# Scaling both banks of a projection pair at once, copying keys earlier, and two longer pauses, in a hybrid decoder block

## The chip, the cores and the metric

The kernel runs on one core of a Trainium2 chip. The metric is the device time of one execution in microseconds (us), the median of three runs of the same program. TensorE (PE) does the matrix products, VectorE (DVE) and ScalarE (ACT) the elementwise work, GpSimd (POOL) issues most of the small copies, and SyncE (SP) issues the weight transfers. Matrix products write to PSUM, which has eight banks; everything else lives in SBUF.

## The reference

A block of a language model on 256 tokens with 16 learned "meta" tokens ahead of them, T = 272 in all, width 2048. One wide projection feeds two branches: gated DeltaNet (16 heads of 128) and forgetting attention (16 heads of 128). Their outputs are mixed by per-channel sigmoid gates, projected, added to the input, and followed by a squared-ReLU MLP of width 8192.

```
u = rms_norm(h, mix_norm_g)
p = u @ w_in                                   # q, k, v | z | b, a | fox q, k, v | f | gate_a, gate_b
qkv = silu(causal_depthwise_conv(p[q, k, v]))  # four taps for each channel
beta, g = sigmoid(b), -exp(a_log) * softplus(a + dt_bias)
w = solve(tril(beta * k k^T * decay) + 1, ...) # the inverted triangular blocks, per head
o = chunked_gated_delta_rule(q, k, v, g, beta)
y_b = forgetting_attention(fox q, k, v, f)
h = h + (sigmoid(gate_a) * (y_a @ w_o_gdn) + sigmoid(gate_b) * (y_b @ w_o_fox)) @ w_out
h = h + square(relu(rms_norm(h) @ w_up)) @ w_down
```

All of it is float32, and the kernel keeps that precision by splitting each operand in a high and a low part.

## The kernel before, in words

The weights are read once, in pieces of 1 MB (`load`, L138, on SP's queue; three buffers). Each half piece is split: ACT writes the high part `wh` (L130, shown as L82), DVE the low part `wl` (L131). PE multiplies three times for each tile of 128 rows and 128 columns: high by high, high by low, low by high (L168 to L170). A pair of 256 columns, two heads, is 96 such products, in two PSUM banks `acc` out of a pool of four. So the pair after next writes to the banks of this pair, and can start only when they have been read.

For q, k and v that reader is `ca` (L465): DVE multiplies the bank by the row `RU` (one over the norm of each token) and writes SBUF. ACT and DVE then do the four taps of the convolution (L466, L470) and the SiLU (L472).

All the small work (convolutions, gates, key products, the triangular inversion, the heads of the delta rule) is written as generators that stand in a list. After each k-tile of a projection `pump()` advances each of them by one `yield`; `pause(n)` waits n k-tiles. So the text of the kernel gives an order of instructions. The kernel is then built with a scheduler that places the instructions anew on each engine by its own costs, so a pause moves instructions by more or less than its count. Each engine runs its own list strictly in order, and an instruction that waits holds back all that stand behind it on its engine.

The places that the change touches:
- `small_columns` (L321): the 48 columns for beta, decay and forget gate (`rawS`), 48 narrow products L338 to L340, then `gates` (L378), with the ten tiny cumulative sums L414 to L423.
- `key_pair` (L612): two heads of keys: convolution, products k k^T (L625, L628), sums of squares (L631, L634).
- `invert` (L518): the diagonal blocks are inverted on DVE (`substitute`), go through DRAM (`dY`) and back, and are joined by small products from L552 on.
- `query_pair` (L695), and `value_head` (L737), one for each of the 16 heads. A value head takes the convolved `vt`, copies it with POOL to `vb` and a part of `kT` to `kb` (`bits`, L90), transposes them on PE (`flip`, L94), and runs a chain of small products: L771, L777, L785, and twice L791, L792, L799, L806. `V` (L758) scales the transposed values. There are 29 such small products for a head, 58 for a pair.

Temporary tiles come from pools by size: ten of 128 columns (`kb` among them), twelve of 272 (`ca`, `cv`, `vt`, `vb`), four of 512.

Of the kernel before, what the change touches and what calls it, by code (L numbers as in the profile page):

```python
# [15 lines left out]
P = 128  # L16
D = 2048
KT = D // P
NM = 16
# [14 lines left out]
def hybrid_block(ctx: ExitStack, tc: tile.TileContext, x, meta_tokens, mix_norm_g, w_in, conv_w, a_log,  # L34
# [46 lines left out]
    def acopy(out, in_, scale=1.0):  # L81
        act.activation(out=out, in_=in_, func=AF.Copy, scale=scale)  # L82
# [5 lines left out]
    def bits(src, shape, name, queue=None):  # L88
        dst = tt(shape, name, F32R)
        (queue or nc.gpsimd).dma_start(out=f(dst), in_=src)  # L90
        return dst
# [30 lines left out]
    def pause(n):  # L122
        for _ in range(n):
            yield
# [196 lines left out]
    def small_columns():  # L321
        rawS = wraw.tile([P, KT, 48], F32, name="rawS", tag="raw")
        wv = win.rearrange("(kt p) n -> p kt n", p=P)
        nc.sync.dma_start(out=rawS[:, :, 0:32], in_=wv[:, :, C_B:C_B + 32])
        nc.sync.dma_start(out=rawS[:, :, 32:48], in_=wv[:, :, C_F:C_F + 16])
        pc = [tt([96, P], f"pc{i}") for i in range(2)]
        cwv = conv_w.rearrange("l t (c p) -> (l t c) p", p=P)
        for i in range(2):
            nc.sync.dma_start(out=pc[i], in_=cwv[i * 96:(i + 1) * 96, :])
        nc.sync.dma_start(out=bc[:, 0, :], in_=a_log.partition_broadcast(P))  # L330
        nc.sync.dma_start(out=bc[:, 1, :], in_=dt_bias.partition_broadcast(P))
        nc.sync.dma_start(out=bc[:, 2, :], in_=fox_f_bias.partition_broadcast(P))
        yield from pause(6)
        wh, wl = split(rawS, KT, 48)
        acc = acc_tile()
        for kt in range(KT):
            o = acc[:48, 0:T]
            pe.matmul(o, wh[:, kt, :], part(u, kt, 0, 0, T), start=(kt == 0), stop=False)  # L338
            pe.matmul(o, wh[:, kt, :], part(u, kt, 1, 0, T), start=False, stop=False)
            pe.matmul(o, wl[:, kt, :], part(u, kt, 0, 0, T), start=False, stop=(kt == KT - 1))  # L340
            if kt == 8:
                ps = ps_tile()
                for i in range(2):
                    pe.transpose(out=ps[:, i * 96:(i + 1) * 96], in_=pc[i], identity=ident[:96, :96])
                acopy(cwT.rearrange("p t c -> p (t c)"), ps[:, 0:192])
            if kt % 2:
                yield
        yield from gates(acc)
# [108 lines left out]
    tasks.append(small_columns())  # L457


    def conv_silu(dst, acc, ct, n, lead):  # L460
        w = [cwT[:, k, ct:ct + 1] for k in range(4)]
        ca, cv = tt([P, T], "ca"), tt([P, T], "cv")
        m = n - lead
        with tc.high_priority():
            dve.tensor_tensor(out=ca[:, 0:n], in0=acc[:, 0:n], in1=RU[:, T - n:T], op=ALU.mult)  # L465
        acopy(cv[:, 0:m], ca[:, lead:n], scale=w[3])  # L466
        for d in range(1, 4):
            yield
            off = max(0, d - lead)
            dve.scalar_tensor_tensor(out=cv[:, off:m], in0=ca[:, lead + off - d:n - d], scalar=w[3 - d],  # L470
                                     in1=cv[:, off:m], op0=ALU.mult, op1=ALU.add)
        act.activation(out=dst, in_=cv[:, 0:m], func=AF.Silu)  # L472
# [45 lines left out]
    def invert():  # L518
        I = big_tile([P, 4352], "I")
        N3 = I[:, 0:1024].rearrange("p (r c) -> p r c", c=32)  # L520
        Y3 = I[:, 1024:2048].rearrange("p (r c) -> p r c", c=32)
        YT = I[:, 2048:4096].rearrange("p (a c) -> p a c", c=64)
        dA = dram.tile([4, HT, 32, 32], F32, name="dA")
        for b in range(4):
            nc.sync.dma_start(out=dA[b].rearrange("a r c -> r a c"), in_=XT3[q[b], :, q[b]])
        nc.sync.dma_start(out=N3, in_=dA.rearrange("b a r c -> (b a) r c"))
        identity(Y3, 32)
        yield from pause(18)
        yield from substitute(N3, Y3, I[:, 4096:4352], 32, P)
        dve.tensor_copy(out=N3, in_=Y3.rearrange("p a b -> p b a"))  # L530
        dY = dram.tile([2, 4, HT, 32, 32], F32, name="dY")
        nc.sync.dma_start(out=dY[0].rearrange("b a r c -> (b a) r c"), in_=Y3)
        nc.sync.dma_start(out=dY[1].rearrange("b a r c -> (b a) r c"), in_=N3)
        pool.memset(YT[0:32, :, 32:64], 0.0)
        for b in range(4):
            nc.sync.dma_start(out=XT3[q[b], :, q[b]], in_=dY[0, b].rearrange("a r c -> r a c"))
            if b < 3:
                cs = slice(32, 64) if b == 1 else slice(0, 32)
                nc.sync.dma_start(out=YT[q[b], :, cs], in_=dY[1, b].rearrange("a r c -> r a c"))
        yield from pause(18)  # L540

        B1 = [I[:, i * 256:(i + 1) * 256].rearrange("p (a c) -> p a c", c=32) for i in range(2)]
        B2 = [I[:, 1024 + i * 512:1536 + i * 512].rearrange("p (a c) -> p a c", c=64) for i in range(2)]
        G4 = HT // 8
        for step in range(G4 + 3):
            g = [step - i if 0 <= step - i < G4 else None for i in range(4)]
            p1 = ps_tile()[:, 0:256].rearrange("p (a c) -> p a c", c=32)
            p2 = ps_tile()[:, 0:256].rearrange("p (a c) -> p a c", c=32)
            p3 = ps_tile().rearrange("p (a c) -> p a c", c=64)

            def mm(o_, a_, b_):
                pe.matmul(o_, a_, b_, start=True, stop=True)  # L552

            def idx(x, i):
                return 8 * g[x] + i


            for i in range(8):
                if g[2] is not None:
                    mm(p3[hi, i, :], XT3[lo, idx(2, i), hi], YT[lo, idx(2, i), :])  # L560
                if g[3] is not None:
                    mm(p3[lo, i, :], B2[g[3] % 2][hi, i, :], XT3[hi, idx(3, i), hi])
            for i in range(8):
                if g[0] is not None:
                    for b in (0, 2):
                        mm(p1[q[b + 1], i, :], XT3[q[b], idx(0, i), q[b + 1]], YT[q[b], idx(0, i), 0:32])
                if g[1] is not None:
                    b1 = B1[g[1] % 2]
                    mm(p2[q[0], i, :], b1[q[1], i, :], XT3[q[1], idx(1, i), q[1]])
                    mm(p2[q[2], i, :], b1[q[3], i, :], XT3[q[3], idx(1, i), q[3]])  # L570
                    mm(p2[q[1], i, :], XT3[q[1], idx(1, i), q[1]], b1[q[1], i, :])
            js = [slice(8 * x, 8 * x + 8) if x is not None else None for x in g]
            if g[0] is not None:
                for b in (1, 3):
                    acopy(B1[g[0] % 2][q[b]], p1[q[b]])
            if g[1] is not None:
                acopy(XT3[q[0], js[1], q[1]], p2[q[0]], scale=-1.0)
                acopy(YT[q[1], js[1], 0:32], p2[q[1]], scale=-1.0)
                acopy(XT3[q[2], js[1], q[3]], p2[q[2]], scale=-1.0)
            if g[2] is not None:  # L580
                acopy(B2[g[2] % 2][hi], p3[hi])
            if g[3] is not None:
                acopy(XT3[lo, js[3], hi], p3[lo], scale=-1.0)
            yield from pause(3)
        done.add("XT")
# [24 lines left out]
        done.add("XTm")  # L610

    def key_pair(hp, accs):  # L612
        for c in range(2):
            h = 2 * hp + c
            yield from conv_silu(kT[:, h, :], accs[c], 16 + h, T, 0)
            if c == 0:
                yield from pause(2)
        yield from pause(4)
# [76 lines left out]
    def query_pair(hp, accs):  # L695
        dst = [QT[:, 2 * hp + c, :] for c in range(2)]
        if "XT" not in done:

            dst = [tt([P, 256], "qt") for c in range(2)]
        for c in range(2):  # L700
            yield from conv_silu(dst[c], accs[c], 2 * hp + c, 260, 4)
            if c == 0:
                yield from pause(2)
        yield from pause(4)
# [31 lines left out]

    def value_head(h, acc):  # L737
        pace = 4
        yield from pause(10 * (h % 2))
        vt = tt([P, T], "vt")  # L740
        yield from conv_silu(vt, acc, 32 + h, T, 0)
        vb = bits(vt[:, NM:T], [P, 256], "vb")
        vs, ks = [tt([P, 3, NM], name, F32R) for name in ("vs", "ks")]
        stack(vs, vt[:, 0:NM], (0, 2))
        stack(ks, kT[:, h, 0:NM], (0, 2))
        kk = [kT[:, h, NM + t * P:NM + (t + 1) * P] for t in range(2)]
        qq = [QT[:, h, t * P:(t + 1) * P] for t in range(2)]
        yield from pause(3)
        yield from until("k", "XT", "XTm")
        kb = bits(kT[:, h, NM:NM + P], [P, P], "kb")  # L750
        ps = ps_tile()
        for t in range(2):
            flip(ps[:, t * P:(t + 1) * P], vb[:, t * P:(t + 1) * P])
# [425 lines left out]
```

## Time and profile before

| | |
|---|---|
| median of three runs | 1991.64 us (1990.89 to 1992.62) |
| the profiled execution | 1992.09 us, of which the span is 1990.3 us |
| mean granted PE clock | 0.997 of 2.4 GHz |
| PE | busy 1966.9 us, 99% of the span |
| DVE | busy 1200.4 us, 60% |
| ACT | busy 1008.2 us, 51% |
| POOL | busy 115.1 us, 6% |
| DMA | 378.77 MB, mean 190 GB/s |

PE works nearly all the time, so the time is what PE has to do and the few places where it waits. The products of the gate columns run from 20.7 us, the key products (L628) from 68.6 to 178.0 us, the joining of the inverted blocks (L552) from 260.4 to 291.8 us, and the value heads (L791) from 381.1 to 542.2 us; forgetting attention, gates and MLP follow. An idle time shown in a row is time in which no product of PE is under way. Products overlap in the pipeline (each is busy for 0.29 us, and the next starts 0.12 us after it), so the next product is later by somewhat more than the idle time shown.

### The profile page before, as it was taken

What the parts mean: (1) busy time and instruction counts of PE and PEld (TensorE: products, weight loads), DVE (VectorE), ACT (ScalarE), POOL (GpSimd) and SP (SyncE); (2) the same over time, 40 slices, a digit from 0 to 9 for tenths busy, and PEclk for the clock granted to TensorE, in tenths of its full rate; (3) what the DMA queues carried; (4) which work ended last, traced back from release to release, by engine and by line L of the source; (5) the groups of instructions that cost most, each with busy time, mean ns of one, the idle gap of its engine ahead of it and who ended that gap; (6) DMA issues with size and microseconds to landing.
All of it is one profiled execution on the core that took longest, in us unless ns stands there. A gap on an engine that the chain in (4) does not pass through costs nothing.

```text
span 1990.3 us, 30185 instructions
## 1 busy us (share of the span) xinstructions
PE 1966.9 (99%) x11974; PEld 1735.0 (87%) x11974; DVE 1200.4 (60%) x2005; ACT 1008.2 (51%) x1797; POOL 115.1 (6%) x168
## 2 busy tenths in 40 slices
PE   8999999999999999999999999999999999999998
PEld 7898999999999998888888888888888888888886
DVE  5786846677546776644444555566655456665555
ACT  5644466556555555444444445555543345554444
POOL 0022100011131110000000000000000000000000
PEclk9999999999999999999999999999999999999999
DMA  6556766544566545656565666666655566666555
GB/s 201 171 162 204 217 179 205 165 140 141 182 210 198 165 165 200 203 190 201 190 201 190 201 243 212 199 188 188 188 191 193 197 194 186 188 186 212 196 197 176
DMA packets 283139, 378.77 MB, mean 190 GB/s; under 512 B 24163, under 2 KB 190406, under 8 KB 282470
## 3 DMA queue, kind: packets, MB, share of 16 engines
q1 hardware_dynamic: 275584, 353.65, 56.3%
q0 software_dynamic: 7200, 22.92, 3.5%
q8 instruction: 94, 1.54, 0.3%
q14 instruction: 47, 0.39, 0.1%
q10 hardware_dynamic: 214, 0.28, 0.0%
HBM read 351.63 MB, written 3.76 MB: 179 GB/s over the span
## 4 chain that ended last, share of the span: by engine, by line
PE 93%; issue 3%; DMA 2%; DVE 1%; ACT 0%; SPq 0%; POOL 0%; POOLq 0%; DVEq 0%; ACTq 0%
PE acc L165 15%; PE acc L183 15%; PE acc L185 15%; PE acc L184 15%; PE acc L170 14%; PE acc L168 7%; PE acc L169 7%; PE ps L94 1%; DVE wl L131 1%; DMA kb<-kT 1%; PE ps L552 0%; DMA rawS<-in_w_in_dram 0%; PE ps L896 0%; PE ps L628 0%; DMA dY<-I 0%
## 5 line engine op out<-in xcount | busy, mean ns | idle before, releaser
L131 DVE TENSOR_TENSOR wl<-raw,wh 128x1024 fp32r<-128x1024 f32 x644 | 787.7, 1224 | 635.1 <-ACT wh L82 631.8
L82 ACT ACTIVATE wh<-raw 128x1024 fp32r<-128x1024 f32 x644 | 682.1, 1060 | 751.8 <-PE acc L185 463.7
L170 PE MATMUL acc<-u,wl 128*128 128x272 f32 (+2 forms) x1536 | 440.5, 290 | 0.6 <-DVE wl L131 0.6
L168 PE MATMUL acc<-u,wh 128*128 128x272 f32 (+1 forms) x1280 | 373.0, 293 | 1.0 <-DVE ca L465 1.0
L169 PE MATMUL acc<-u,wh 128*128 128x272 f32 (+1 forms) x1280 | 371.8, 291 | 0.0
L165 PE MATMUL acc<-v,wh 128*128 128x512 f32 x1024 | 355.8, 396 | 0.0
L170 PEld LDWEIGHTS acc<-u,wl 128*128 128x128 f32 x1536 | 289.6, 189 | 3.2 <-DVE wl L131 1.2
L170 PE MATMUL acc<-v,wl 128*128 128x256 f32 x1024 | 279.3, 279 | 0.0
L168 PEld LDWEIGHTS acc<-u,wh 128*128 128x128 f32 x1280 | 241.6, 189 | 2.3 <-DVE ca L465 1.5
L169 PEld LDWEIGHTS acc<-u,wh 128*128 128x128 f32 x1280 | 243.0, 190 | 0.7 <-issue 0.2
L165 PEld LDWEIGHTS acc<-v,wh 128*128 128x128 f32 x1024 | 189.5, 188 | 42.8
L184 PE MATMUL acc<-wl,h1h 128*128 128x512 f32 x504 | 196.1, 389 | 0.0
L185 PE MATMUL acc<-wh,h1l 128*128 128x512 f32 x504 | 196.1, 389 | 0.0
L170 PEld LDWEIGHTS acc<-v,wl 128*128 128x128 f32 x1024 | 192.9, 188 | 3.5
L183 PE MATMUL acc<-wh,h1h 128*128 128x512 f32 x504 | 176.3, 389 | 0.0
L185 PE MATMUL acc<-wh,u 128*128 128x512 f32 x384 | 151.6, 395 | 0.0
L184 PE MATMUL acc<-wl,u 128*128 128x512 f32 x384 | 151.1, 394 | 0.0
L183 PE MATMUL acc<-wh,u 128*128 128x512 f32 x384 | 139.2, 396 | 0.0
L183 PEld LDWEIGHTS acc<-wh,h1h 128*128 128x128 f32 x504 | 94.6, 188 | 19.8
L185 PEld LDWEIGHTS acc<-wh,h1l 128*128 128x128 f32 x504 | 94.6, 188 | 19.6
L184 PEld LDWEIGHTS acc<-wl,h1h 128*128 128x128 f32 x504 | 94.6, 188 | 19.4
L165 PE MATMUL acc<-u,wh 128*128 128x512 f32 x256 | 89.5, 395 | 0.0
(378 smaller groups left out, 2387.8 us busy)
## 6 DMA issues: line engine op xcount, KB each, us to landing
raw<-in_w_in_dram SPq DMA_DIRECT2D x142, 1024.0 KB, 5.2
raw<-in_w_down_dram SPq DMA_DIRECT2D x66, 1024.0 KB, 5.2
raw<-in_w_up_dram SPq DMA_DIRECT2D x64, 1024.0 KB, 5.8
raw<-in_w_o_gdn_dram SPq DMA_DIRECT2D x16, 1024.0 KB, 5.2
raw<-in_w_o_fox_dram SPq DMA_DIRECT2D x16, 1024.0 KB, 5.4
raw<-in_w_out_dram SPq DMA_DIRECT2D x16, 1024.0 KB, 5.3
vb<-vt POOLq DMA_DIRECT2D x32, 128.0 KB, 2.2
tb<-tl POOLq DMA_DIRECT2D x16, 208.0 KB, 2.2
```

The costliest lines, as they stand in the source:

```text
L82: act.activation(out=out, in_=in_, func=AF.Copy, scale=scale)
L94: pe.transpose(out=out.bitcast(F32R), in_=in_, identity=identr)
L131: dve.tensor_tensor(out=wl, in0=raw, in1=f(wh), op=ALU.subtract)
L165: pe.matmul(accs[c][:, 0:2 * n].rearrange("p (a n) -> p a n", a=2), wh[:, s], m[kt // 8][:, kt % 8, :, n0:n1], start=(kt == 0), stop=False)
L168: pe.matmul(o, wh[:, s], part(m, kt, 0, n0, n1), start=(kt == 0), stop=False)
L169: pe.matmul(o, wh[:, s], part(m, kt, 1, n0, n1), start=False, stop=False)
L170: pe.matmul(o, wl[:, s], part(m, kt, 0, n0, n1), start=False, stop=(kt == KT - 1))
L183: pe.matmul(accs[t], a, wh, start=(kt == 0), stop=False)
L184: pe.matmul(accs[t], a, wl, start=False, stop=False)
L185: pe.matmul(accs[t], b, wh, start=False, stop=(kt == nkt - 1 - (last if t else 0)))
```

## The change

Four edits. `pause(6)` before the split of the gate columns becomes `pause(11)`. The product `ca` is taken out of `conv_silu` into a function `normalized`, and both banks of a key pair or query pair are scaled ahead of the first convolution; a value head scales its bank ahead of its own `pause(10 * (h % 2))`. `pause(18)` between the transfers of the inverted blocks and their products becomes `pause(20)`. In `value_head` the copy `kb` is written some steps earlier, ahead of `pause(3)`.

```diff
@@ small_columns
-        yield from pause(6)
+        yield from pause(11)
         wh, wl = split(rawS, KT, 48)
@@
-    def conv_silu(dst, acc, ct, n, lead):
-        w = [cwT[:, k, ct:ct + 1] for k in range(4)]
-        ca, cv = tt([P, T], "ca"), tt([P, T], "cv")
-        m = n - lead
+    def normalized(acc, n):
+
+        ca = tt([P, T], "ca")
         with tc.high_priority():
             dve.tensor_tensor(out=ca[:, 0:n], in0=acc[:, 0:n], in1=RU[:, T - n:T], op=ALU.mult)
+        return ca
+
+    def conv_silu(dst, ca, ct, n, lead):
+        w = [cwT[:, k, ct:ct + 1] for k in range(4)]
+        cv = tt([P, T], "cv")
+        m = n - lead
         acopy(cv[:, 0:m], ca[:, lead:n], scale=w[3])
@@ invert
-        yield from pause(18)
+        yield from pause(20)
@@ key_pair
+        cas = [normalized(acc, T) for acc in accs]
         for c in range(2):
             h = 2 * hp + c
-            yield from conv_silu(kT[:, h, :], accs[c], 16 + h, T, 0)
+            yield from conv_silu(kT[:, h, :], cas[c], 16 + h, T, 0)
@@ query_pair
+        cas = [normalized(acc, 260) for acc in accs]
         for c in range(2):
-            yield from conv_silu(dst[c], accs[c], 2 * hp + c, 260, 4)
+            yield from conv_silu(dst[c], cas[c], 2 * hp + c, 260, 4)
@@ value_head
         pace = 4
+        ca = normalized(acc, T)
         yield from pause(10 * (h % 2))
         vt = tt([P, T], "vt")
-        yield from conv_silu(vt, acc, 32 + h, T, 0)
+        yield from conv_silu(vt, ca, 32 + h, T, 0)
         vb = bits(vt[:, NM:T], [P, 256], "vb")
         vs, ks = [tt([P, 3, NM], name, F32R) for name in ("vs", "ks")]
         stack(vs, vt[:, 0:NM], (0, 2))
         stack(ks, kT[:, h, 0:NM], (0, 2))
+        yield from until("k")
+        kb = bits(kT[:, h, NM:NM + P], [P, P], "kb")
         kk = [kT[:, h, NM + t * P:NM + (t + 1) * P] for t in range(2)]
         qq = [QT[:, h, t * P:(t + 1) * P] for t in range(2)]
         yield from pause(3)
         yield from until("k", "XT", "XTm")
-        kb = bits(kT[:, h, NM:NM + P], [P, P], "kb")
```

The number of instructions stays the same on every engine; their order changes on PE, DVE, ACT and, slightly, POOL, and not on SP. In the changed kernel L464 is L465 of before, L475 is L470, L789 is L780, L794 is L785, L800, L801, L808 and L815 are L791, L792, L799 and L806.

On PE, at the start of the program, both kernels have the same rows; the products of the gate columns follow the first 48 products of the key columns:

```order
L169 MATMUL acc<-u_140,wh 128x272
L170 MATMUL acc<-u_140,wl 128x272
L338 MATMUL acc<-u_140,wh 48x272
L339 MATMUL acc<-u_140,wh 48x272
L340 MATMUL acc<-u_140,wl 48x272
```

Nothing moved there on PE.

On DVE, at the fourth key pair, the rows of before from the copy `th` (L443) of the gates on; the banks 180, 506 and 507 are those of the first and second pair:

```order
L443 COPY th_573<-ps_569 32x272
L465 TENSOR_TENSOR ca_604<-acc_180,RU_139 128x272
L465 TENSOR_TENSOR ca_696<-acc_506,RU_139 128x272
L465 TENSOR_TENSOR ca_738<-acc_507,RU_139 128x272
L470 SCALAR_TENSOR_TENSOR cv_605<-ca_604,cwT_154,cv_605 128x271
```

And the rows of the changed kernel from the same copy on; here acc_469 and acc_470 are the second pair's banks, acc_682 and acc_683 the third pair's:

```order
L443 COPY th_615<-ps_611 32x272
L637 SCALAR_TENSOR_TENSOR jk_1043,ssk_174<-ps_1039,ident_89 16x16
L640 SCALAR_TENSOR_TENSOR jk_1043,ssk_174<-ps_1039,ident_89 128x128
L131 TENSOR_TENSOR wl_901<-raw_898,wh_900 128x1024
L637 SCALAR_TENSOR_TENSOR jk_1051,ssk_174<-ps_1047,ident_89 16x16
L640 SCALAR_TENSOR_TENSOR jk_1043,ssk_174<-ps_1039,ident_89 128x128
L640 SCALAR_TENSOR_TENSOR jk_1051,ssk_174<-ps_1047,ident_89 128x128 x2
L644 TENSOR_SCALAR nrk_177<-ssk_174 128x3x2
L464 TENSOR_TENSOR ca_696<-acc_469,RU_139 128x272
L464 TENSOR_TENSOR ca_698<-acc_470,RU_139 128x272
```

The first pair's two banks are scaled long before; the second pair's wait behind the sums of squares of the first pair's keys and a weight split.

On PE, in the value columns, where a new bank is first written: before, the second bank of a pair starts 36 products after the first, behind this group of 12 small products:

```order
L94 MATMUL ps_5466<-identr_94,vb_5408 128x128 x2
L94 MATMUL ps_5466<-identr_94,vs_5410 48x128
L805 MATMUL ps_5491<-y_5433,kd_5162 128x128
L806 MATMUL ps_5491<-y_5433,kq_5228 128x128
L771 MATMUL ps_5499<-vnm1_4208,xs1_4212 48x128
L777 MATMUL ps_5503<-QT_3030,kT_170 128x128 x2
L806 MATMUL ps_5521<-y_5456,kq_5051 128x128
L799 MATMUL ps_5526<-rhs_5461,XT_171 128x128
L94 MATMUL ps_5530<-identr_94,ks_5411 48x128
L94 MATMUL ps_5530<-identr_94,kb_5464 128x128
L168 MATMUL acc_5617<-u0_140,wh_5620 128x272
```

And in the changed kernel the end of a group of 24 small products that stands ahead of the first product of a pair:

```order
L800 MATMUL ps_5636<-S_5567,kT_170 128x128
L801 MATMUL ps_5636<-S_5567,QT_3030 128x128
L94 MATMUL ps_5642<-identr_94,vb_5578 128x128 x2
L94 MATMUL ps_5642<-identr_94,vs_5580 48x128
L800 MATMUL ps_5669<-S_5597,kT_170 128x128
L801 MATMUL ps_5669<-S_5597,QT_3030 128x128
L794 MATMUL ps_5675<-ptm0_4209 128x128
L815 MATMUL ps_5708<-y_5634,kq_5230 128x128
L808 MATMUL ps_5713<-rhs_5639,XT_171 128x128
L94 MATMUL ps_5717<-identr_94,ks_5581 48x128
L94 MATMUL ps_5717<-identr_94,kb_5586 128x128
L168 MATMUL acc_5896<-u0_140,wh_5900 128x272
```

The group that held both the flips of `vb` and of `kb` stood inside a pair and stands now, twice as long, at its end.

On DVE, at the same place, the rows of the changed kernel that end with the scaling of the bank (acc_5340) which acc_5896 is to take over:

```order
L803 SCALAR_TENSOR_TENSOR rhs_5562<-ps_5559,neG_166,V_5090 128x128
L131 TENSOR_TENSOR wl_6040<-raw_6037,wh_6039 128x1024
L818 SCALAR_TENSOR_TENSOR S_5597<-S_5399,eGl_163,ps_5594 128x128
L821 TENSOR_TENSOR QT_3030<-ps_5594,QT_3030 128x128
L789 SCALAR_TENSOR_TENSOR kq_5609<-ps_5606,cst_176,DT_168 128x128 x2
L782 SCALAR_TENSOR_TENSOR ptm0_4209<-ps_5602,kds_164,ptm0_4209 16x128
L101 TENSOR_TENSOR vs_5580<-vt_5539,vs_5580 128x16
L101 TENSOR_TENSOR ks_5581<-kT_170,ks_5581 128x16
L803 SCALAR_TENSOR_TENSOR rhs_5639<-ps_5636,neG_166,V_5368 128x128
L766 CAST vnm1_4208<-ps_5642 48x128
L767 TENSOR_TENSOR V_5646<-ps_5642,nrk_177 128x256
L464 TENSOR_TENSOR ca_5649<-acc_5340,RU_139 128x272
```

Before, no weight split stands in the rows of DVE between the flips of `vb` and the scaling. Now `wl_6040` stands ahead of it, and `ca_5649` stands behind `V_5646`, which needs the copy `vb_5578`.

## Rows read from the trace of the kernel before

**Rows 1.** The page, part 1: busy time and share of the span.

```profile
PE 1966.9 (99%) x11974; PEld 1735.0 (87%) x11974; DVE 1200.4 (60%) x2005; ACT 1008.2 (51%) x1797; POOL 115.1 (6%) x168
```

**Rows 2.** Waits of PE: us in total, times, longest.

```profile
PE ps L94 <- DMA kb<-kT: 2.9, 6, 1.1
PE acc L338 <- ACT wh L82: 1.9, 1, 1.9
PE ps L552 <- DMA I<-dY: 1.3, 1, 1.3
PE acc L168 <- DVE ca L465: 1.0, 2, 0.9
...
PE acc L170 <- DVE wl L131: 0.6, 2, 0.3
...
PE ps L625 <- ACT kT L472: 0.5, 1, 0.5
```

**Rows 3.** Timeline of PE at the gate columns: start, duration, idle time before.

```profile
18.36 0.29 PE L169 MATMUL acc<-u,wh 128*128 128x272 f32 x1
18.48 0.29 PE L170 MATMUL acc<-u,wl 128*128 128x272 f32 x1
20.68 0.33 PE L338 MATMUL acc<-u,wh 128*48 128x272 f32 x1 [1.91 <-ACT wh L82]
```

**Rows 4.** Timeline of ACT at the same place.

```profile
19.78 0.84 ACT L82 ACTIVATE wh<-rawS 128x768 fp32r<-128x768 f32 x1 [2.25 <-DMA rawS<-in_w_in_dram]
```

**Rows 5.** Windows: stretch, length, engines' busy time (instructions), granted clock, DMA share, GB/s.

```profile
21.00:24.40 3.40, 2.87 (x14) 2.40 (x13) 3.40 (x6) 1.62 (x3) 0.00 (x0) 0.50 0.75 207
...
409.20:412.60 3.40, 3.40 (x28) 3.40 (x29) 1.93 (x4) 2.36 (x7) 0.00 (x0) 1.00 0.00 0
```

**Rows 6.** Timeline of DVE at the fourth key pair.

```profile
62.40 0.43 DVE L443 COPY th<-ps 32x272 f32<-32x272 f32 x1 [2.85 <-PE ps L441]
62.75 1.11 DVE L465 TENSOR_TENSOR ca<-acc,RU 128x272 f32<-128x272 f32 x3
```

**Rows 7.** Timeline of PE at the fourth key pair.

```profile
63.23 0.39 PE L168 MATMUL acc<-u,wh 128*128 128x272 f32 x1 [0.87 <-DVE ca L465]
```

**Rows 8.** Window of one value pair, from one `kb` flip to the next.

```profile
409.20:428.20 19.00, 18.69 (x154) 18.39 (x154) 13.58 (x34) 11.53 (x37) 2.14 (x4) 1.00 0.41 132
```

**Rows 9.** Groups of instructions in the value columns: busy us, mean ns of one, idle before.

```profile
L131 DVE TENSOR_TENSOR wl<-raw,wh 128x1024 fp32r<-128x1024 f32 x26 | 31.8, 1222 | 5.3 <-ACT wh L82 5.3
L82 ACT ACTIVATE wh<-raw 128x1024 fp32r<-128x1024 f32 x27 | 28.6, 1059 | 5.9 <-PE acc L169 5.6
L470 DVE SCALAR_TENSOR_TENSOR cv<-ca,cwT,cv 128x271 f32<-128x271 f32 (+2 forms) x36 | 18.0, 499 | 3.7 <-ACT cv L82 2.3
...
L780 DVE SCALAR_TENSOR_TENSOR kq<-ps,cst,DT 128x128 f32<-128x128 f32 x26 | 8.4, 347 | 2.4 <-PE ps L777 1.9
...
L812 DVE TENSOR_TENSOR QT<-ps,QT 128x128 f32<-128x128 f32 x25 | 7.1, 283 | 0.7 <-PE ps L806 0.7
```

**Rows 10.** Timeline of ACT, POOL and DVE in the second value pair.

```profile
440.90 0.43 ACT L472 ACTIVATE vt<-cv 128x272 f32<-128x272 f32 x1 [0.39 <-ACT wh L82]
...
441.63 0.54 POOL L90 DMA_DIRECT2D vb<-vt  x1 [6.69 <-ACT vs L82]
...
445.26 0.28 DVE L757 CAST vnm<-ps 48x128 fp32r<-48x128 f32 x1 [1.13 <-PE ps L94]
...
445.47 0.41 DVE L758 TENSOR_TENSOR V<-ps,nrk 128x256 f32<-128x256 f32 x1
...
445.52 0.54 POOL L90 DMA_DIRECT2D kb<-kT  x1 [3.36 <-PE ps L94]
...
447.01 0.43 DVE L465 TENSOR_TENSOR ca<-acc,RU 128x272 f32<-128x272 f32 x1
```

**Rows 11.** Timeline of PE in the same pair, at the `kb` flip.

```profile
447.40 0.28 PE L94 MATMUL ps<-identr,kb 128*128 128x128 f32 x1 [0.39 <-DMA kb<-kT]
```

**Rows 12.** The copies `vb` in the value columns: issue to landing.

```profile
DMA to landing us min/median/max: 2.0/2.1/3.3
```

## The prediction

> **What bounds the kernel now.** I read the page's busy times first: PE is busy for 1966.9 of 1990.3 us [rows 1], so only a wait of PE, or a lower clock, can be gained or lost. The change leaves the number of products as it is. Then the waits of PE: those that the change could touch are the six waits for the copy `kb` (2.9 us idle), the wait for the split of the gate columns (1.9), the wait for the inverted blocks (1.3), and in the key columns the waits for `ca` (1.0), for a weight split (0.6) and for `kT` (0.5) [rows 2]. That is 8.2 us idle, the most that could vanish. A wait delays PE by more than its idle time: products start 0.12 us apart [rows 3], yet each keeps PE busy for 0.29, so 0.17 us of a wait lies under the product still running. I add 0.15 for each wait.
>
> **Gate columns, first edit: nothing.** The wait at 20.68 stands right behind the 48th key product: ACT's split waited for the transfer of `rawS`, started at 19.78, and PE waited 1.91 us for it [rows 3, 4]. On PE the rows of the changed kernel here are the same, so the narrow products still stand ahead of the other key products, and SP's order is the same. The pause moves only a weight split on ACT and DVE ahead of the split of `rawS`, into time in which both wait for the transfer (ACT was idle for 2.25 us) [rows 4]. I take 0. Were the wait gone it would be 1.9 us and part of the slow clock behind it; were the moved split in the way, 1.06 us, one `wh` [rows 9].
>
> **Inverted blocks, third edit: nothing.** The first joining product stands at the same place among the projection's products in both orders, and DVE and SP have the same rows ahead of it. Its 1.3 us [rows 2] stays. Bounds: 1.3 us gained, if the longer pause kept PE busy until the transfer lands, and as much lost.
>
> **Key pairs, second edit.** Before, DVE read three banks one after the other behind the copy L443, and the next pair's first product waited 0.87 us for one of them [rows 6, 7]. The waits for `ca`, `wl` and `kT` are five with 2.1 us idle together [rows 2], with 0.15 each some 2.9 us. I let all of them go. In the new order the scaling of the second pair's bank stands behind the first pair's sums of squares and a weight split, and the fourth pair's first product needs it. From the end of the product that frees the weight buffer (two products ahead of that place): `wh` 1.06, `wl` 1.22 [rows 9], one short and three longer rows of sums (at most 0.35 each, as the like row L780 [rows 9]) and one `ca` of 0.43 [rows 10] make 4.0; DVE starts a row 0.07 before the one ahead ends (445.26 + 0.28 against 445.47 [rows 10]), which takes some 0.4 off: 3.6. PE has two products and six small ones to do meanwhile, 0.9 us. So it waits about 2.6 us. Some 80 products later the next bank's weight split stands behind three scalings, twelve taps of 0.43 and four other rows; I put that at 1.2 us, between nothing and 2.5. Sum: -2.9 + 2.6 + 1.2 = +0.9 us; bounds -2.9 and +3.
>
> **Value heads, second and fourth edit: the term that decides.** One pair takes 19.0 us and holds 154 products, 96 of the projection and 58 small ones [rows 8]. 96 by 0.125 are 12.0; with 0.45 of wait taken off, 6.55 us are left for 58, 0.113 each. Before, the copy `kb` was issued only when a flip of PE set its buffer free (POOL idle for 3.36 us until then), some 1.9 us ahead of its use, and PE waited 0.39 us [rows 10, 11]. In the new order every second `kb` is issued long before its use, and those waits go: 2.9 us idle and six times 0.15, 3.8 us in all. But the other head's copies are now used in the group of 24 small products that stands at each pair's end, and the first product of the next pair waits for `ca`, which on DVE stands behind `V`, which needs `vb`.
>
> I walk that group from the product that frees the weight buffer, 26 ahead of the pair's end (t = 0). ACT's `wh` ends at 1.06; DVE's `wl`, two `kq`, three taps and L812 follow (1.22, 0.35, 0.50, 0.28 less 0.07 each [rows 9]): 4.3. ACT must first make the next `wh`, free when PE is two products from the end (24 products and 6 small ones, 3.7), so until 4.75; then a small `S` and `vt` with 0.43 [rows 10]: 5.4. The copy was issued 0.30 us behind the end of `vt` (440.90 + 0.43 against 441.63 [rows 10]) and lands 2.1 us later [rows 12]: 7.8. Three flips, then L757 to L758 0.21, `V` 0.34 and `ca` 0.43 [rows 10]: 9.1. PE, if it never waited, would be there after 26 products and 30 small ones, 3.25 + 3.39 = 6.6. So it waits 2.5 us. A second path says nearly the same without the copy: on DVE the `wl` behind that second `wh` and the eleven rows from there to `ca` (0.2 to 0.4 each, 2.8 together) end at 8.7, a wait of 2.1. Since part of the 0.113 of a small product is itself waiting on ACT and DVE, which would then fall into the same gap, I take 2.0. The order shows this group at six pair ends: 12.0 us. Bounds for one: 0.5, what a pair loses now, and 3.7, with the longest landing of 3.3 [rows 12].
>
> Value heads: 12.0 - 3.8 = +8.2 us. The query pairs get nearly the same order; 0. The order behind the value heads is the same; 0.
>
> **Sum.** 0.9 + 8.2 = +9.1 us. The profiled execution took 1992.1 us, so the changed kernel's would take 2001.2; it lay 0.45 above the median of the runs, 1991.64. Forecast: 2000.5 us.
>
> **A rule on the clock.** Behind the 1.9 us wait the granted clock was 0.50, the 1.2 GHz level, for 3.4 us [rows 2, 5]; behind the `kb` wait of 1.1 us it stayed 1.00 [rows 2, 5]. Waits of 2.0 to 2.5 us lie on the wrong side of these two. The Trainium skill (TensorE: Matmul & The Clock Gate, section "HAM oscillation") says that a wait between groups of products that recurs with each tile can lower the clock anew each time. By it six such places would cost more than their waits, which is the third rival; by the row at 1.1 us they would not. The rows here lie on both sides.
>
> **Rivals.** First, the other side: the copies come early and nothing takes the place of the waits. It decides at the pair's end: if small products on PE run close behind their inputs, so that `vb` is there when its flip comes, `ca` is done ahead of the next pair. For it: POOL is idle most of the time, and DVE is busy for 13.6 of 19.0 us [rows 8], so there is room. Against it: the 2.1 us of the copy can't shrink, and only 14 small products stand ahead of the flip in that group. Then the 3.8 us go, and 2.0 of the 2.9 in the key columns: 1991.6 - 5.8 = about 1986.
>
> Second, the change does not do what it says: gate columns and inversion don't move, as above, and POOL issues `vb` and `kb` in the same sequence as before, so at the pair's end one wait is put in the place of another, some 0.7 us for six `kb` waits of 0.63: 1991.6 + 0.4 + 0.9 for the key columns, about 1993. For it: `ca` ended at 447.44, as the flip of `kb` began at 447.40 [rows 10, 11], so both were due together already. The Trainium skill (Perfetto Trace Analysis, "Identifying Performance Opportunities") says that a gap which recurs on the engine that should be full can mean too few buffers for the next tile. The change adds none, so by that rule the gap would stay; the row of POOL that waits for a flip agrees.
>
> Third, the clock: each of the six waits brings 3.4 us at 0.50, which costs 1.7 us more: 2000.5 + 10 = about 2011.
>
> **How the numbers follow.** Forecast (pair ends wait 1.2 to 2.8 us): 0.48, its own range 1995 to 2006. First rival 0.23, second 0.21, third 0.08. The range, 1986 to 2011, takes in the first rival's middle, the sum of the lower bounds being lower still, and the third's. A measurement of this kernel tells 0.2%, 4 us, from no change: faster is below 1987.7, slower above 1995.6. The first rival is faster in most of its cases (0.20 of 0.23), the forecast and the third are slower (0.54 of 0.56), the rest lies between: 0.20, 0.26, 0.54.
>
> **What would show it.** Right: PE's waits list six for `ca` or `vb` at the value pairs, each above 1 us, no wait for `kb` of 0.3 us, a value pair of some 20.5 us, one wait of over 2 us for `ca` ahead of the fourth pair, and the 1.9 and 1.3 us waits as they were. Wrong: value pairs of 18.6 us (first rival) or 19.1 (second), a granted clock under 0.9 in the value columns (third), or the gate columns' products without a wait.

## The result, and the profile after

The changed kernel took 2004.54 us, median of four runs (2002.48 to 2005.83), against 1991.27 us before (1990.39 to 1992.62): a ratio of 1.0062, 95% interval 1.0046 to 1.0078. It is slower by 13.3 us; forecast were 9. The profiled execution has a span of 2003.1 us against 1990.3.

PE's busy time and its waits, as in [rows 1, 2], in the page and the waits of PE of the changed kernel:

```profile
PE 1973.8 (99%) x11974; PEld 1739.5 (87%) x11974; DVE 1200.8 (60%) x2005; ACT 1007.9 (50%) x1797; POOL 113.2 (6%) x168
```

```profile
PE acc L168 <- DVE ca L464: 2.6, 1, 2.6
PE ps L800 <- DVE QT L821: 2.2, 5, 0.5
PE acc L338 <- ACT wh L82: 1.6, 1, 1.6
PE ps L94 <- DVE vs L101: 1.6, 4, 0.4
PE ps L786 <- ACT S L82: 1.4, 4, 0.4
PE ps L94 <- DVE ptm L782: 1.3, 1, 1.3
PE ps L557 <- DMA I<-dY: 1.2, 1, 1.2
...
PE ps L94 <- DVE rhs L803: 0.7, 1, 0.7
PE ps L94 <- DMA vb<-vt: 0.7, 1, 0.7
```

The waits for `kb` are gone. The one for the gate columns (1.6) and the one for the inverted blocks (1.2) are still there. New are a single wait of 2.6 us for `ca` and a whole family in the value columns. PE's busy time rose by 6.9 us with the same products: a product at the lower clock counts as busy for 0.43 us instead of 0.29, and products that stand apart overlap less (a value pair of the changed kernel has PE busy for 19.25 us, one of before for 18.69 [rows 8]).

Where the time was lost: I compared the start of each projection product in the two traces, since there are equally many in one order. The changed kernel is 4.7 us behind at the start of the value columns (350.21 us against 345.48), 11.9 behind after the last value head (612.78 against 600.88), and 12.75 at the last product. So the value columns lost 7.2 us and what stands ahead of them 4.7.

First columns. The timeline of PE at the fourth key pair, which answers to [rows 7], and three windows (length, engines' busy time, granted clock, DMA share, GB/s), which answer to [rows 5]:

```profile
72.39 0.71 PE L634 MATMUL ps<-kT 128*128 128x128 f32 x4
75.67 0.36 PE L168 MATMUL acc<-u,wh 128*128 128x272 f32 x1 [2.56 <-DVE ca L464]
```

```profile
63.10:66.50 3.40, 3.40 (x16) 3.33 (x16) 0.85 (x6) 1.34 (x4) 0.00 (x0) 0.50 0.45 152
66.50:69.90 3.40, 3.40 (x17) 3.35 (x15) 1.22 (x1) 0.28 (x3) 0.00 (x0) 0.50 0.26 40
76.76:80.17 3.41, 3.41 (x18) 3.41 (x17) 3.41 (x10) 0.60 (x3) 3.33 (x4) 0.50 0.84 250
```

The wait is as long as forecast, 2.56 us against 2.6. Behind it the clock was granted at half, 1.2 GHz, for 3.41 us. The ten cumulative sums of the gates end at 64.3 us, and around them the clock was at half for 6.8 us here, 3.4 us before.

Value columns. One window from a flip of `vb` to the next pair's, to set beside [rows 8]:

```profile
465.34:485.79 20.45, 19.25 (x154) 18.58 (x155) 14.33 (x37) 11.83 (x38) 2.13 (x4) 1.00 0.41 123
```

The same 154 products take 20.45 us instead of 19.0 to 19.2, at a full clock. The timeline of PE through the group of small products at the end of that pair:

```profile
482.51 0.30 PE L780 MATMUL ps<-vnm,xs 128*48 128x128 f32 x1
483.16 0.71 PE L786 MATMUL ps<-QT,kT 128*128 128x128 f32 x4 [0.34 <-ACT S L82]
483.73 0.49 PE L808 MATMUL ps<-rhs,XT 128*128 128x128 f32 x2
484.71 0.49 PE L800 MATMUL ps<-S,kT 128*128 128x128 f32 x2 [0.49 <-DVE QT L821]
485.03 0.39 PE L801 MATMUL ps<-S,QT 128*128 128x128 f32 x2
485.79 0.34 PE L94 MATMUL ps<-identr,vb 128*128 128x128 f32 x2 [0.37 <-DVE vs L101]
...
487.34 0.23 PE L94 MATMUL ps<-identr,kb 128*128 128x128 f32 x1
487.41 0.36 PE L168 MATMUL acc<-u,wh 128*128 128x272 f32 x1
```

And what the other engines did then, from the timelines of ACT, POOL and DVE:

```profile
481.88 1.05 ACT L82 ACTIVATE wh<-raw 128x1024 fp32r<-128x1024 f32 x1
482.83 0.27 ACT L82 ACTIVATE S<-ps 128x128 f32<-128x128 f32 x1
482.99 0.44 ACT L477 ACTIVATE vt<-cv 128x272 f32<-128x272 f32 x1
...
483.72 0.54 POOL L90 DMA_DIRECT2D vb<-vt  x1 [12.83 <-ACT QT L82]
```

```profile
482.97 1.23 DVE L131 TENSOR_TENSOR wl<-raw,wh 128x1024 fp32r<-128x1024 f32 x1 [0.38 <-ACT wh L82]
484.37 0.28 DVE L821 TENSOR_TENSOR QT<-ps,QT 128x128 f32<-128x128 f32 x1
...
485.58 0.18 DVE L101 TENSOR_TENSOR vs<-vt,vs 128x16 fp32r<-128x16 f32 x1
...
486.76 0.42 DVE L464 TENSOR_TENSOR ca<-acc,RU 128x272 f32<-128x272 f32 x1
```

The copies `vb` of the value columns, from issue to landing:

```profile
DMA to landing us min/median/max: 1.9/2.0/2.9
```

Read PE's three waits downwards. L786 waits for `S`, which stands on ACT behind the weight split `wh`. L800 waits for `QT`, which stands on DVE behind the weight split `wl`. At the third, the flip of `vb`, the profile names `vs`, which ended at 485.76, but it is the copy that PE waits for: `vb` landed at 485.66, and the flip starts 0.14 us later. In the value columns of the thirteen profiles of this document 38 flips of `vb` wait for more than 0.15 us, and every one starts 0.14 us behind the landing, whatever the profile names. The copy is late because `vt` stands on ACT behind the same `wh`. `ca` ends at 487.18, and PE comes to the next pair at 487.41, so `ca` makes it wait for nothing.

### The profile page after: what moved, and what is told of

The parts are those of the page before. It is cut to its first block, busy times and chain, and to the rows that moved or that the text cites. A ratio compares the mean times of both kernels' runs of the same rounds, so it can differ in the third digit from the quotient of the medians.

```text
span 2003.1 us, 30212 instructions
## 1 busy us (share of the span) xinstructions
PE 1973.8 (99%) x11974; PEld 1739.5 (87%) x11974; DVE 1200.8 (60%) x2005; ACT 1007.9 (50%) x1797; POOL 113.2 (6%) x168
## 4 chain that ended last, share of the span: by engine, by line
PE 92%; DVE 3%; DMA 3%; ACT 1%; issue 1%; SPq 0%; POOL 0%; POOLq 0%; DVEq 0%; ACTq 0%
PE acc L183 15%; PE acc L185 15%; PE acc L184 14%; PE acc L170 14%; PE acc L165 14%; PE acc L168 7%; PE acc L169 7%; PE ps L94 1%; DVE wl L131 1%; ACT wh L82 1%; PE ps L557 0%; PE ps L634 0%; DMA rawS<-in_w_in_dram 0%; PE ps L905 0%; DMA dY<-I 0%
```

## The experiments

Ratios are against the kernel before, run on the same chip, with their 95% intervals. In the comparisons by profile "behind" means the start of the same projection product. The mean granted clock is on record for every execution; the share that it lacks, times the span, is used below as an estimate of the time that the lower clock cost. In every profile 5 to 7 us at half lie behind the last product, where they cost nothing; they are in the estimate of every kernel alike.

**The pause of the gate columns alone.**

```diff
-        yield from pause(6)
+        yield from pause(11)
         wh, wl = split(rawS, KT, 48)
```

> The kernel before with the pause ahead of the split of the gate columns at 11 instead of 6, and nothing else. Theory A (the pause alone delays the gates, so that the first key products, their sums of squares and a scaling stand one behind the other ahead of the fourth key pair): PE waits once over 2 us for a scaling or a weight split near 75 us, the granted clock is at 0.50 for more than the two stretches of 3.4 us of before, and the key columns end 4 to 5 us later; time 1995 to 1997 us, value pairs of 19.05 us as before. Rival B (the loss ahead of the value columns comes from scaling both banks of a key pair at once): key columns as before, 1991 us.

Measured: 1997.73 us, ratio 1.0039 (1.0026 to 1.0053). The wait of 2.42 us ahead of the fourth key pair is there, at 70.71 us, though the profile names another row of DVE, `cst`, and there is a second of 3.86 us for a weight split at 86.34 us; at each the clock was at half. Value pairs took 19.1 us. The pause alone costs, and theory A holds for this part, though the second wait is one that the changed kernel does not have.

**The value heads' scaling alone.**

```diff
         pace = 4
+        ca = normalized(acc, T)
         yield from pause(10 * (h % 2))
         vt = tt([P, T], "vt")
-        yield from conv_silu(vt, acc, 32 + h, T, 0)
+        yield from conv_silu(vt, ca, 32 + h, T, 0)
```

> The kernel before with the scaling of a value head's bank taken ahead of its pause; the key copy stays where it was, key and query pairs and the pauses too. Theory A (this edit alone puts the small products together at the pair's end, where each waits for ACT or DVE): a value pair takes 20.3 us or more, with a group of 20 small products at its end; 7 to 10 us more, 1998 to 2001 us. Rival C (the early key copy does it, by changing which buffers are free): value pairs of 19.05 us, 1991 us.

Measured: 2004.85 us, ratio 1.0086 (1.0062 to 1.0110). Theory A, and more than it said: PE's waits at the flips of `vb` were 1.5 to 2.0 us at five pairs. Two rows of the waits of PE:

```profile
PE ps L94 <- DMA vb<-vt: 6.3, 4, 2.0
...
PE ps L94 <- DVE rhs L800: 3.4, 2, 1.8
```

The profiled execution took 2014.8 us, the three others 2004.1 to 2004.9. In it the clock fell to half for 6.8 us behind four of these waits; the others, at a mean granted clock of 0.995 to 0.996 against 0.989, can't have had four such falls. A window of 6 us behind one of the waits, and the whole pair that it belongs to:

```profile
463.00:469.00 6.00, 6.00 (x28) 5.77 (x29) 3.27 (x9) 1.91 (x7) 0.00 (x0) 0.50 0.01 1
462.93:486.80 23.87, 22.02 (x154) 21.44 (x155) 14.49 (x36) 11.78 (x39) 2.14 (x4) 0.86 0.34 105
```

Less the 3.4 us that 6.8 us at half cost, the pair takes 20.5 us, as long as in the changed kernel. So the early scaling alone makes a pair longer by 1.4 us, and the clock comes on top.

**The early key copy alone.**

```diff
+        yield from until("k")
+        kb = bits(kT[:, h, NM:NM + P], [P, P], "kb")
         kk = [kT[:, h, NM + t * P:NM + (t + 1) * P] for t in range(2)]
...
-        kb = bits(kT[:, h, NM:NM + P], [P, P], "kb")
```

> The kernel before with the key copy of a value head some steps earlier, and nothing else. Theory A: the small products stay spread over the pair, and the six waits for the copy become shorter or go: 0 to 3.8 us less, 1987.5 to 1991 us, value pairs of 18.5 to 19.0 us. Rival C: value pairs of over 20 us and 7 us more, 1998 us.

Measured: 1993.59 us, ratio 1.0016 (1.0006 to 1.0025). No wait for `kb`, and no gain: value pairs of 19.35 us against 19.1. In the waits of PE the scaling has taken its place, six times 0.40 us (the other two are before 110 us, as in [rows 2]), and a wait for an ACT row has come up:

```profile
PE acc L168 <- DVE ca L465: 3.4, 8, 0.9
PE ps L778 <- ACT QT L82: 1.7, 6, 0.3
```

Neither theory gave this sign, and the longer pairs are some 1.5 us of the 3.4 by the medians. By the mean granted clock of the executions, 0.9968 against 0.9975, some 1.5 more are clock. Rival C falls: the loss of 7 us is not the copy's.

**Everything but the value heads.** The changed kernel with `value_head` as it was before.

```diff
         pace = 4
-        ca = normalized(acc, T)
         yield from pause(10 * (h % 2))
         vt = tt([P, T], "vt")
-        yield from conv_silu(vt, ca, 32 + h, T, 0)
+        yield from conv_silu(vt, normalized(acc, T), 32 + h, T, 0)
...
-        yield from until("k")
-        kb = bits(kT[:, h, NM:NM + P], [P, P], "kb")
...
+        kb = bits(kT[:, h, NM:NM + P], [P, P], "kb")
```

> The changed kernel with the value heads as they were before (their scaling behind the pause, the key copy late); both longer pauses and the scaling of both banks of key and query pairs are in. Theory A: the loss of the first columns alone, 4 to 5 us, with value pairs of 19.05 us: 1995 to 1997 us. Rival C, if the value columns lose by what stands ahead of them: 2003 us.

Measured: 1993.46 us, ratio 1.0023 (1.0011 to 1.0034), value pairs of 19.1 us. The 13.3 us of the whole change split in 3.2 (by the medians) to 4.5 (by the ratio) for the first columns and the rest for the value heads. The first columns run here in the order of the changed kernel, with the wait at 70.93 us (2.42) and the clock at half behind it:

```profile
71.08:74.49 3.41, 3.41 (x16) 3.41 (x17) 3.41 (x12) 1.50 (x4) 3.41 (x4) 0.50 0.28 64
```

But in this execution no other product ran at half clock: 3.4 us in all against 13.7 in the profile of the changed kernel (and 6.8 in that of before), and at the start of the value columns it was 0.65 us ahead of the kernel before, not 4.7 behind. The profile of one execution tells the first columns to no better than this. The granted clocks say more: their mean is 0.9963 over these seven executions and 0.9975 over the seventeen of the kernel before, which is 7.4 and 4.9 us. By this estimate 2.5 us of what the first columns cost is clock.

**Both edits of the value heads, and nothing else.** The kernel before with the `value_head` of the changed kernel.

> The kernel before with both edits of the value heads (scaling ahead of the pause, early key copy) and neither longer pause nor the scaling of two banks at once for key and query pairs. Theory A (the value heads carry 7 us by themselves, by waits of less than 1.5 us inside a group of small products, at a granted clock of 1.00): value pairs of 20.45 us, 7 us more by the end of the value columns, 1997 to 1999 us. Rival D (the two edits of the value heads add up: the loss of the scaling alone, with the clock at 0.50 at each pair, stays): value pairs of over 22 us and 2003 us or more.

Measured: 1998.92 us, ratio 1.0039 (1.0026 to 1.0053); value pairs of 20.46 us; from the start of the value columns to behind the last value head it lost 8.8 us on the kernel before. Theory A; rival D falls: with the early copy the waits are 0.3 to 0.8 us (one of 1.4), and all but one of them left the clock alone. The pairs are as long as with the early scaling alone, less its falls of the clock; in place of one wait of 1.5 to 2.0 us stand several short ones. Why the early copy brings this order was not tried by itself. The mean granted clock of the four executions is 0.9972 against 0.9973 for the fifteen of the kernel before, so these 8 us are not the clock's. The changed kernel's four executions have 0.9950: by the same estimate some 4 to 5 of its 13.3 us are clock, and the rest is about what the value heads lose.

**The scaling four k-tiles early instead of ten**, with the early copy.

```diff
-        yield from pause(10 * (h % 2))
+        yield from pause(6 * (h % 2))
+        ca = normalized(acc, T)
+        yield from pause(4 * (h % 2))
...
```

> The kernel before with the early key copy, and with the second head's scaling taken 4 k-tiles ahead of its convolution instead of 10: the small products then stand in groups of 7 and 9 and not of 24. Theory A (what costs is a long group of dependent products, not the early scaling as such): no waits for the key copy, value pairs of 18.5 to 19.0 us, 0 to 4 us less than before, 1987 to 1991 us. Rival E (any early scaling of the second bank costs, since DVE then does it ahead of what PE needs): value pairs over 19.3 us, 1993 us or more.

Measured: 1992.83 us, ratio 1.0011 (1.0002 to 1.0020). With the shorter groups the pair takes 19.45 us, between before and after. No wait in the value columns is over 0.3 us, but each pair has two, of 0.2 and 0.3 us:

```profile
PE ps L785 <- ACT QT L82: 1.7, 6, 0.3
PE ps L814 <- DVE V L766: 1.4, 6, 0.2
```

The loss is 0.35 us a pair and not 1.4, which fits theory A's long group; but the scaling is also less early here, and no kernel separates the two. The level is not theory A's: the pair lies in rival E's range, over 19.3 us, and the time just under its 1993.

**One `kq` row less on DVE in the changed kernel.**

```diff
-        for t in range(2):
+        for t in range(1):
             dve.scalar_tensor_tensor(out=kq[:, t, :], in0=ps[:, t * P:(t + 1) * P],
...
-            pe.matmul(ps[:, 0:P], kq[:, t, :], y, start=True, stop=True)
+            pe.matmul(ps[:, 0:P], kq[:, 0, :], y, start=True, stop=True)
```

> The changed kernel, which leaves out the scaling of one of the two k q^T blocks of each value head on DVE (the first block's is used twice): a DVE row of 0.28 us less ahead of the flips of vb in the group at the pair's end, with all else in nearly the same order. Theory F (DVE's list is what the group waits for): a value pair is 0.25 to 0.35 us shorter, 20.1 to 20.2 us. Rival G (the landing of the copy vb sets it): at most 0.1 us shorter, and the wait at the flip goes over to the copy.

Measured: 2001.38 us in the one execution; value pairs of 20.4 to 20.7 us where the clock is full, against 20.45: nothing gained. In the waits of PE the longest wait for `QT` fell from 0.49 to 0.30 us, and for most flips the profile now names the copy:

```profile
PE ps L94 <- DMA vb<-vt: 2.6, 4, 0.8
...
PE ps L786 <- ACT S L82: 2.2, 5, 0.4
...
PE ps L800 <- DVE QT L821: 1.5, 5, 0.3
```

Rival G: the landing of the copy sets the flip. Here `vs` had ended some 0.5 to 0.8 us ahead of the flip at the pairs behind the first two, and still each flip starts 0.14 us behind the landing of `vb`, as in the changed kernel.

**The changed kernel with the pause at 6 again.**

> The changed kernel with the pause ahead of the gate columns back at 6. Theory A (the pause alone brings the wait of 2.5 us ahead of the fourth key pair): no such wait, value pairs as in the changed kernel (20.45 us), 1997 to 2001 us, 3 to 7 us under the changed kernel. Rival H (scaling both banks of a key pair at once does its share): a wait of over 1 us for a scaling stays ahead of the fourth key pair, 2002 us or more.

Measured: 2004.31 us, ratio 1.0073 (1.0057 to 1.0088), no less than the changed kernel. The wait at the fourth key pair is gone, but PE waits 3.55 us at 97.82 us for a weight split. So the pause of 11 costs by itself (first experiment) and yet taking it back from the whole gains nothing. Rival H's sign, with another place and another releaser than it named.

**Both banks of key and query pairs scaled at once, alone.**

```diff
+        cas = [normalized(acc, T) for acc in accs]
         for c in range(2):
...
-            yield from conv_silu(kT[:, h, :], accs[c], 16 + h, T, 0)
+            yield from conv_silu(kT[:, h, :], cas[c], 16 + h, T, 0)
...
```

The query pairs are changed in the same way.

```diff
...
+        cas = [normalized(acc, 260) for acc in accs]
         for c in range(2):
-            yield from conv_silu(dst[c], accs[c], 2 * hp + c, 260, 4)
+            yield from conv_silu(dst[c], cas[c], 2 * hp + c, 260, 4)
```

> The kernel before with both banks of key and query pairs scaled ahead of the first convolution, and nothing else. Theory H (this edit alone moves the loads of ACT's function tables ahead of a weight split, as in the changed kernel with pause 6, where PE waited 3.55 us at 98 us): a wait of over 2 us for a weight split between 80 and 105 us, the clock at 0.50 behind it, value pairs of 19.05 us; 2 to 5 us more, 1993 to 1996 us. Rival A (only the pause of the gate columns costs in the first columns): no such wait, 1989 to 1992 us.

Measured: 1994.43 us, ratio 1.0013 (1.0003 to 1.0022). Theory H: the same wait of 3.55 us, at 98.11 us. The timeline of ACT ahead of it:

```profile
92.62 1.28 ACT L477 ACT_TABLE_LOAD   x1
...
94.25 0.92 ACT L82 ACTIVATE cv<-ca,cwT 128x272 f32<-128x272 f32 x2
95.19 1.28 ACT L374 ACT_TABLE_LOAD   x1
96.48 0.63 ACT L374 ACTIVATE DT<-DT 128x512 f32<-128x512 f32 x1
97.02 1.04 ACT L82 ACTIVATE wh<-raw 128x1024 fp32r<-128x1024 f32 x1
```

Two loads of ACT's function table of 1.28 us each, one for the SiLU of the keys and one back to the exponential of the decay, stand between two weight splits.

**The pause of the inverted blocks alone.**

```diff
-        yield from pause(18)
+        yield from pause(20)
```

> The kernel before with the pause ahead of the products of the inverted blocks at 20 instead of 18, and nothing else. Theory A: the first of them stands at the same place, the wait for the blocks stays between 0.8 and 1.5 us, 1990 to 1992 us. Rival I (the pause keeps PE busy until the blocks are there): no wait for the blocks, 1 us less.

Measured: 1993.08 us, ratio 1.0005 (0.9996 to 1.0015). The wait for the blocks is 0.98 us. Nothing, as theory A had it. No product of this profiled execution ran at half clock, and it was the fastest of its ten, 1988.6 us.

**One more buffer of 128 columns.**

```diff
-TMP_BUFS = {"t128": 10, "t272": 12, "t512": 4}
+TMP_BUFS = {"t128": 11, "t272": 12, "t512": 4}
```

> The kernel before with eleven buffers instead of ten for temporary tiles of 128 columns, from which the key copies come; the text is else the same. Theory J (the key copy is late because its buffer is, and behind it the scaling of the bank is due at the same time): no waits for the key copy, in their place waits of 0.3 to 0.45 us for the scaling, value pairs of 19.0 to 19.4 us, 1989 to 1992 us. Rival K (the copy was the only thing late): no wait of PE at the value pairs, value pairs of 18.5 us, 3 us less.

Measured: 1990.11 us, ratio 0.9991 (0.9981 to 1.0001). Theory J to the letter: no wait for the key copy, six waits of 0.39 to 0.41 us for the scaling, pairs of 19.1 us. No kernel here is faster than the one before by more than can be measured.

## Why the prediction was right

The time lies where it was forecast, and the edits acted where it was said. On the way to the size two steps failed, and there the result is luck, as told below.

- **Direction and size.** Slower by 9.1 us was forecast and 13.3 measured; 2004.54 lies in the forecast's own range. (1991.64 and 9.1 are 2000.7; the forecast says 2000.5.)
- **Gate columns and inverted blocks: nothing.** Both waits stayed (1.91 to 1.60, 1.29 to 1.17 us). Over the thirteen profiles the first was 0.5 to 2.0 us with the pause of 6 and 0.8 to 2.4 with that of 11, the second 0.6 to 1.5, and the pause of 20 alone is 1.0005. Right.
- **The wait ahead of the fourth key pair, 2.6 us.** 2.56 in the changed kernel, 2.42 in two others with the same rows. The releaser is the one that was forecast. But both ends of the walk came later than worked out: from the start of the split at 71.49 us PE was out of work after 1.6 us instead of 0.9 (six small products are twelve rows of the trace, see below) and the bank was free after 4.2 instead of 3.6. The two misses cancel, so the tenth of a microsecond is luck.
- **The second wait there, 1.2 us.** It did not come. Wrong.
- **What the first columns cost, +0.9 us: mis-sized.** The same first columns without the value heads' edits cost 0.23% (0.11 to 0.34%), 4.5 us, or 3.2 by the medians. The five short waits went, as forecast. I had kept the halved clock for a rival in the value columns and left it out of the sum where a wait of 2.6 us was in it: it stood at that wait in all four kernels that have one, 3.41 us at half, some 1.7 us each. With it and without the second wait the sum is 1.4 us (-2.9 + 2.6 + 1.7). The granted clocks above put some 2.5 us on the clock; the rest is within what the executions differ by.
- **Value pairs of some 20.5 us.** 20.45. Per pair 2.0 us of waits less the 0.63 of the `kb` waits were forecast, 1.37 net; 1.3 to 1.4 us were lost at each inner pair, and 7.2 between the ends of the value columns for 8.2 forecast.
- **What PE waits for there: the path right, the place wrong.** By its own sign, six waits of over 1 us for `vb` or `ca`, it fails: at the inner pairs there are three waits of 0.34 to 0.49 us inside the group, the last of them for `vb`, and `ca` is in time. The walk along ACT and DVE held: from the product that frees the weight buffer, which ends at 477.53, `vb` landed after 8.1 us (7.8 worked out) and `ca` ended after 9.7 (9.1).
- **PE's own way in that walk: mis-counted, and there the size is luck.** To the pair's end 6.6 us were worked out, and it took 9.9. The walk took 30 small products at 0.113 us, the price of one of the 58 of [rows 8]. Those 58 are rows of the trace, in which most small products are two: L786 is a loop of two products and stands above as x4, while the two flips of `vb` are x2. On this way the trace has 44 rows. 3.25 and 44 by 0.113 are 8.2 us; the three waits, with some 0.15 each as in the prediction, are the rest. At 8.2 the same walk leaves a wait of 0.9 for `ca`, six of them less 3.8 are 1.6, and the sum would have been 2.5 us instead of 9.1. The waits inside the group, which the walk had not, made up for those at the end, which it had. Outside the group the 24 rows took 0.11 us each, as before (20.45 less 12.0 and 5.82, by 24); the 34 inside took 0.17, in 5.82 us from 481.59 to 487.41.
- **First rival (early copies gain).** The copies do come early, and two kernels show what follows: with the early copy alone or one buffer more the `kb` waits vanish and the scaling, due at the same time, costs as much. That both were due together was the second rival's row [rows 10, 11]. The Trainium skill's rule that a recurring gap can mean too few buffers (Perfetto Trace Analysis, "Identifying Performance Opportunities") held for the gap it was read from, as one buffer more removed the waits for `kb`. Six waits of 0.40 us for the scaling took their place, and nothing was gained.
- **Third rival (the clock at each pair).** It did not happen in the changed kernel, whose waits there are short, but in one execution of the kernel with the early scaling alone, whose waits were 1.5 to 2.0 us. The rule of the Trainium skill that such waits can lower the clock anew each time (TensorE: Matmul & The Clock Gate, "HAM oscillation") describes that execution, 6.8 us at 0.50 behind each of four waits; the three others of the same kernel were 10 us faster.

## What to carry to other kernels

Here a chain of small products is threaded through a stream of large ones, and it cost 1.4 us a pair to put its links together, though their inputs were asked for earlier: put together, each link waited for the queue of another engine, and each of the three waits had a weight split ahead of it in such a queue. Before removing a short wait, look what else is due at the same moment: the scaling was due within a tenth of a microsecond of the copy `kb`, and two kernels without the waits for the copy gained nothing. Take a price and the count that it is multiplied by from the same place: a product of the text can be two rows of the trace. Where the profile names an engine for a wait, set the start beside the landings of the copies as well. A walk along the engines' queues with the durations of the trace told which copy and which queue matter, but its ends were 0.3 to 0.7 us off even where the count was right, and a wait is the difference of two ends. Add what a long wait can do to the clock.

## What the runs showed of the hardware

- Whether and how long the clock falls differs between executions. Seven profiles with the first columns in the order of before had 0, 3.4, 6.8 (three times) and 10.2 us (twice) at half clock in the first 110 us; three in the order of the changed kernel had 3.4, 6.8 and 13.7. That is up to 5 us of time, about as much as executions of one kernel differ by.
- The length of a wait alone does not tell whether the clock falls. Behind the wait of 2.4 to 2.6 us ahead of the fourth key pair it was at half in four of four profiles, and at the waits of 3.55 and 3.86 us for a weight split in three of three. Behind the wait for the split of the gate columns it fell in seven of thirteen: these waits were 1.1 to 2.0 us, while at 1.88 us (one more buffer) and at 2.37 us (everything but the value heads) it stayed up. At the value pairs it fell behind four of five waits of 1.5 to 2.0 us in the one profile that has them, and behind none of the five first-pair waits of 1.1 to 1.6 us in other profiles. In the value columns of all other profiles there were two stretches of 3.4 us in all, right behind waits of 0.6 and 0.7 us.
- A flip of `vb` that waits for its copy starts 0.14 us behind the landing, 38 times of 38, also where the profile names an instruction of DVE.
- A load of ACT's function table takes 1.28 us, longer than a weight split of 1.04, and with two of them between two splits PE waited 3.55 us.
